# One meta product per block, unread products at the start, and the causal table behind the values' remainder

## The chip, the core and the metric

The kernel runs on one core of a Trainium2 chip. The core has five engines that run side by side, each through its own list of instructions in order: TensorE (PE in the profile, its weight loads PEld), VectorE (DVE), ScalarE (ACT), GpSimd (POOL) and SyncE (SP), which here issues the DMAs. The metric is the device time of one execution in microseconds, as the median of several runs.

## The reference

Two decoder layers over 16 meta tokens and 1024 tokens of width 1024. Each layer normalises its input and projects it to queries, keys, values and gates. One half of the heads does sliding-window attention (window 128; the 16 meta tokens are visible to everyone; a sink logit per head), the other half is an mLSTM, a matrix memory that runs over chunks of tokens. Both are gated, joined and projected back.

```
scores = where(mask, q @ [k_meta, k_band].T * scale, -1e30)
probs  = exp(scores - m) / (sum + exp(sink - m))
ya     = probs @ [v_meta, v_band] * silu(ag)
C_t    = f_t * C_{t-1} + i_t * k_t v_t^T          # mLSTM, per chunk:
S      = q k^T * exp(D - m_t)                     # D is causal: -1e30 above the diagonal
h      = (inter * q C_in + S v) / max(|den|, exp(-m_t))
y      = x + concat(ya, norm(h) * sigmoid(mo) * silu(mgate)) @ w_out
```

The output is the last 1024 tokens, in float32.

## The kernel before, in words

Tokens are cut into nine tiles: tile 0 with the 16 meta tokens, tiles 1 to 8 with 128 tokens each. To keep float32 accuracy, every operand of a large product is split into a high part in the TensorE's rounded format (a copy by ScalarE) and a remainder (a subtraction by VectorE or GpSimd); a product is then three products: high with high, high with remainder, remainder with high (mm3, L196, and the parts at L237).

A layer runs through these stages.

**Start** (kv_tasks). In the first layer the rows of x are loaded tile by tile, squared and summed on ScalarE (first_norm, L340), scaled on VectorE (L298), transposed by TensorE into PSUM (norm_half, L306), copied into H as high part by ScalarE (L310) and as remainder by VectorE (L311). The gain of the norm is spread over all partitions by two products with a row of ones (L504, into two banks G). The four pairs of key and value weights are split on ScalarE (L169) and VectorE (L170). Then each tile is projected (projN, L196).

**Attention** (att_tasks), eight head pairs j by eight blocks b of 128 queries, 64 blocks a layer. A block goes through four steps that are spread over three of its successors: s1 computes the scores of both heads of the pair into S and their softmax into a tile P (ScalarE exponentials at L753, scaling at L758); s2 transposes P with TensorE into the single PSUM bank T: at L775 the 2 x 16 columns that belong to the meta tokens, at L777 the two bands. ScalarE and VectorE split the bands into HL (L784, L786) and the meta part into one of two tiles ptm (L785, L787). s3 starts the output in the single PSUM bank O (L806), s4 adds the meta part with two products of 128 columns, one per head, with weights VM that are zero for the other head's rows (L818), and for b > 1 two products with the differences of neighbouring values (L818, from a band that GpSimd cuts at L797). ScalarE and VectorE then add the halves of O (L825, L827). Between the steps, products of the projections for queries and gates (L237) are woven in by a fixed rule, and the order of TensorE's instructions is pinned to the order in which they are written.

VM is written by v_meta: the values of the meta tokens are copied four times under one another by DMA and multiplied with a column that is one for the rows of a head (hrow).

**Recurrence** (m_tasks), four heads by nine chunks: sa splits the values of a chunk (V, high part at L1015 by ScalarE, remainder at L1016 by GpSimd), turns the keys, updates the state C and computes the decayed scores; the decays come as a table EB by DMA, and mask_eb (L995) adds the causal table tri to one chunk's part of EB on GpSimd. sb and sc_ make the output. Beside it run the projections of the next head. Here a scheduler chooses the order on each engine, from priorities and its own estimate of when things are ready.

**Output projection** (L1324): 16 groups of rows of w_out, streamed in and split.

## Time and profile before

| | before |
|---|---|
| median of 3 runs | 1912.39 us (1911.38 to 1912.49) |
| the profiled execution | 1913.58 us |
| its span in the trace | 1911.9 us |
| TensorE busy | 1892.1 us (99%) |
| VectorE / ScalarE / GpSimd busy | 54% / 55% / 51% |
| instructions | 36057 |

The profile gives each engine's busy time, the chain of work that ended last, groups of instructions by line, and what an engine waited for. A line of the timeline has the start and the length in microseconds, the engine, the line of the kernel, the operation with the tile that it writes and the tiles that it reads, shapes, and how many instructions were merged; in brackets stands how long the engine sat idle before it and who ended that. A product of TensorE lasts longer than the distance to the next one's start, because products overlap.

### The profile page before, as it was taken

How to read it: one execution, taken by the hardware profiler on the slowest of the kernel's cores; microseconds unless marked ns; L12 is line 12 of the kernel's file. 1: busy time of each engine (PE TensorE's matmuls, PEld its weight loads, DVE VectorE, ACT ScalarE, POOL GpSimd, SP SyncE). 2: the span in 40 equal slices, each digit the busy share in tenths (PEclk: the TensorE clock that was granted, in tenths of full speed). 3: DMA queues.
4: the chain of work that ended last, by engine and by line, in shares of the span. 5: the costliest groups of instructions: out<-in, count | busy, mean ns of one | idle time of the engine just before them, and what ended most of it. 6: DMA issues, size and time to landing. Idle time of an engine off the chain costs nothing.

```text
span 1911.9 us, 36057 instructions
## 1 busy us (share of the span) xinstructions
PE 1892.1 (99%) x12779; PEld 1791.3 (94%) x12779; DVE 1035.6 (54%) x2876; ACT 1052.5 (55%) x3131; POOL 984.5 (51%) x1337
## 2 busy tenths in 40 slices
PE   8999999999999999999999999999999999999999
PEld 7999999999999999877789999999999999998887
DVE  8666767657362543443445677675573636336211
ACT  6577877656453544633334778776554545446221
POOL 3665865446545454651325657654565554546342
PEclk9999999999999999999999999999999999999999
DMA  4111111212212221554540111112122121216543
GB/s 156 29 48 44 39 48 50 57 44 56 64 41 64 56 59 45 180 163 157 176 125 23 48 50 35 54 48 56 49 56 60 52 73 35 63 59 204 161 145 131
DMA packets 152422, 148.29 MB, mean 78 GB/s; under 512 B 16665, under 2 KB 125505, under 8 KB 152242
## 3 DMA queue, kind: packets, MB, share of 16 engines
q1 hardware_dynamic: 152242, 145.98, 26.2%
q8 instruction: 101, 1.65, 0.4%
q14 instruction: 79, 0.65, 0.1%
HBM read 122.59 MB, written 23.29 MB: 76 GB/s over the span
## 4 chain that ended last, share of the span: by engine, by line
PE 85%; DVE 4%; DMA 4%; issue 3%; POOL 3%; ACT 2%; SPq 0%; POOLq 0%; ACTq 0%; DVEq 0%
PE pj L196 32%; PE pj L237 22%; PE pss L1324 6%; PE pj L1324 4%; PE po L1324 4%; PE S L731 3%; PE O L818 3%; PE po L1003 2%; PE pss L1003 2%; DMA raw<-in_w_out_dram 2%; PE O L806 2%; PE T L777 1%; PE pj L221 1%; PE pt L1003 1%; DVE t L949 1%
## 5 line engine op out<-in xcount | busy, mean ns | idle before, releaser
L196 PE MATMUL pj<-H,RING 128*128 128x384 f32 (+2 forms) x3312 | 559.4, 322 | 0.3 <-ACT t L967 0.3
L196 PEld LDWEIGHTS pj<-H,RING 128*128 128x128 f32 x3312 | 521.8, 188 | 2.9 <-ACT t L967 0.5
L170 POOL TENSOR_TENSOR RING<-raw,RING 128x512 fp32r<-128x512 f32 (+1 forms) x192 | 255.5, 1335 | 115.1 <-ACT RING L169 112.8
L237 PE MATMUL pj<-RING,H 128*128 128x256 f32 (+1 forms) x1920 | 269.3, 286 | 0.3 <-ACT u L541 0.3
L237 PEld LDWEIGHTS pj<-RING,H 128*128 128x128 f32 x1920 | 242.4, 189 | 0.7 <-ACT u L541 0.6
L237 PE MATMUL pj<-H,RING 128*128 128x384 f32 (+2 forms) x1296 | 239.2, 324 | 0.0
L196 PE MATMUL pj<-RING,H 128*128 128x256 f32 x1536 | 209.6, 287 | 3.9 <-DVE w1k L205 1.8
L237 PEld LDWEIGHTS pj<-H,RING 128*128 128x128 f32 x1296 | 201.1, 188 | 0.0
L196 PEld LDWEIGHTS pj<-RING,H 128*128 128x128 f32 x1536 | 193.7, 191 | 6.3 <-DVE w1k L205 2.2
L188 POOL TENSOR_TENSOR RING<-raw,RING 128x512 fp32r<-128x512 f32 x85 | 110.9, 1311 | 154.6 <-ACT RING L187 137.6
L187 ACT ACTIVATE RING<-raw 128x512 fp32r<-128x512 f32 x128 | 80.8, 633 | 177.6 <-DMA raw<-in_w_out_dram 167.2
L169 ACT ACTIVATE RING<-raw 128x512 fp32r<-128x512 f32 (+1 forms) x196 | 122.6, 626 | 46.1 <-DMA raw<-in_w_in_dram 34.6
L1016 POOL TENSOR_TENSOR p<-u,p 128x258 fp32r<-128x258 f32 x64 | 47.2, 738 | 147.5 <-ACT p L1015 146.0
L797 POOL TENSOR_SCALAR_AFFINE_SELECT p<-p 128x512 fp32r<-128x512 f32 x112 | 71.6, 640 | 96.6 <-DVE p L786 96.2
L1324 PE MATMUL pss<-RING,H 128*128 128x512 f32 x384 | 120.3, 394 | 0.0
L753 ACT ACTIVATE t<-S,mx 128x145 f32<-128x145 f32 x256 | 93.6, 368 | 36.5 <-DVE mx L750 32.0
L1324 PE MATMUL pj<-RING,H 128*128 128x512 f32 x352 | 110.3, 395 | 0.0
L972 DVE SCALAR_TENSOR_TENSOR t<-t,pj 128x384 f32<-128x384 f32 (+2 forms) x48 | 24.6, 512 | 156.8 <-ACT t L971 156.8
L831 POOL TENSOR_TENSOR u<-u,w1k 128x128 f32<-128x128 f32 x128 | 60.3, 471 | 92.2 <-DVE w1k L827 85.1
L949 DVE SCALAR_TENSOR_TENSOR t<-u,cw,t 128x384 f32<-128x384 f32 (+1 forms) x144 | 106.1, 737 | 2.2
L188 DVE TENSOR_TENSOR RING<-raw,RING 128x512 fp32r<-128x512 f32 x43 | 34.6, 806 | 124.5 <-ACT RING L187 124.5
L758 ACT ACTIVATE t<-t,mx 128x144 f32<-128x144 f32 x256 | 91.9, 407 | 4.5 <-DVE mx L755 3.9
(366 smaller groups left out, 3890.3 us busy)
## 6 DMA issues: line engine op xcount, KB each, us to landing
raw<-in_w_out_dram SPq DMA_DIRECT2D x128, 256.0 KB, 3.0
raw<-in_w_in_dram SPq DMA_DIRECT2D x100, 256.0 KB, 2.8
raw<-in_w_in_dram SPq DMA_DIRECT2D x192, 128.0 KB, 2.3
spool<-u SPq DMA_DIRECT2D x56, 192.0 KB, 1.9
p<-x SPq DMA_DIRECT2D x24, 256.0 KB, 3.8
t<-spool SPq DMA_DIRECT2D x30, 192.0 KB, 3.6
p<-spool SPq DMA_DIRECT2D x26, 192.0 KB, 3.6
u<-em SPq DMA_DIRECT2D x8, 576.0 KB, 6.5
```

Source lines behind the costliest of these rows:

```text
L169: sc.activation(hi, raw[:, :, 0:o], AF.Copy)
L170: eng.tensor_tensor(lo, raw[:, :, 0:o], hi, op=ALU.subtract)
L187: sc.activation(hi, raw, AF.Copy)
L188: (eng or (ve if i > 8 and i % 2 else gp)).tensor_tensor(lo, raw, hi, op=ALU.subtract)
L196: last = pin(pe.matmul(out, a, b, start=(i == 0), stop=(i == n - 1)))
L237: pin(pe.matmul(out(), x, y, start=(k + i == 0), stop=(k == n - 1 and i == 2)))
L753: sc.activation(P[:p, 145 * h:145 * h + 145], S[:p, h, 1 + 127 * h:146 + 127 * h], AF.Exp, bias=mx[:p, 0, h:h + 1], accum_out=mx[:p, 1, h: ...
L758: sc.activation(Pn, Pn, AF.Copy, scale=mx[:p, 2, h:h + 1])
L797: gp.affine_select(OW, HL, [[0, 4], [1, 128]], ALU.is_ge, 0.0, base=0, channel_multiplier=-1)
L949: ve.scalar_tensor_tensor(z, RAW[:, t0 + i:t0 + i + n], wcol(i), z, ALU.mult, ALU.add)
L1003: pin(f(*a, **k))
L1324: pin(pe.matmul(ps[:p, :], a, b, start=(i + n == 0), stop=(i == 15 and n == len(terms) - 1)))
```

## The change

Six edits, told in the order of the program.

1. At the start of the first layer seven products are added whose results nobody reads: five of 128 columns with the row of ones ahead of the two that make G, and two copies of those of 512 columns behind them, all into a bank of their own (spare).
2. The four remainders of the first layer's key and value weights are made on GpSimd instead of VectorE.
3. VM holds one weight tile per key head instead of two: the high parts of the values in its left half, the remainders in the right, with the meta values at rows 0 to 15, 32 to 47, 64 to 79 and 96 to 111 and zeros between. The multiplications with hrow go, and so does the clearing of VM.
4. ptm is 256 columns wide, 128 for each head, and zero where a row does not belong to that head. P has a gap of 16 cleared columns between the heads' parts, so that the transposed meta part is 48 rows long, head 0 at rows 0 to 15 and head 1 at 32 to 47. The copy and the subtraction into ptm are done once per head (2 x 16 rows) instead of once (32 rows).
5. In s4 one product of 256 columns takes the place of the two of 128 columns.
6. In sa the causal table is added to the next chunk's decays after the remainder of the present chunk's values, on the same engine, and not before.

```diff
@@ kv_tasks
+                spare = bank("pj")
+                for i in range(5):
+                    pe.matmul(spare[:, 0:128], one, one, start=True, stop=True)
                 for i in range(2):
                     pe.matmul(G[i], one, gr[0:1, 512 * i:512 * i + 512], start=True, stop=True)
+                for i in range(2):
+                    pe.matmul(spare, one, gr[0:1, 512 * i:512 * i + 512], start=True, stop=True)
...
-                             for i in range(4)])
+                             for i in range(4)], gp)
...
-            for i in range(4):
-                ve.tensor_scalar(VM[:, i // 2, i % 2, :], ident, 0.0, None, ALU.mult)
@@ v_meta
-            x = w1k()[0:64, 0:128]
+            x = w1k()[:, 0:128]
+            ve.memset(x, 0.0)
             for i in range(4):
-                sy.dma_start(x[16 * i:16 * i + 16], VR[:16, 0])
+                sy.dma_start(x[32 * i:32 * i + 16], VR[:16, 0])
             vs = x.rearrange("p (v c) -> p v c", v=2)
-            for h in range(2):
-                hi, lo = [VM[0:64, :, h, c:c + 64] for c in (0, 64)]
-                sc.activation(hi, vs, AF.Copy, scale=hrow[0:64, h:h + 1])
-                ve.scalar_tensor_tensor(lo, vs, hrow[0:64, h:h + 1], hi, ALU.mult, ALU.subtract)
+            sc.activation(VM[:, :, 0:64], vs, AF.Copy)
+            ve.tensor_tensor(VM[:, :, 64:128], vs, VM[:, :, 0:64], op=ALU.subtract)
@@ s1
+                ve.memset(P[:, 145:161], 0.0)
@@ s2
-                tm = X[0:32, 256:256 + p]
-                pin(pe.transpose(tm, P[:p, 129:161], ident[:p, :p]))
+                tm = X[0:48, 256:384]
+                pin(pe.transpose(tm, P[:, 129:177], ident))
...
-                    taken = sc.activation(pm[0:32, 0:p], tm, AF.Copy).ins
+                    meta = [(tm[32 * h:32 * h + 16], *(pm[o:o + 16, 128 * h:128 * h + 128]
+                                                       for o in (32 * h, 64 + 32 * h))) for h in range(2)]
+                    for x, hi, lo in meta:
+                        taken = sc.activation(hi, x, AF.Copy).ins
                     ve.tensor_tensor(HL[:, 256:512], X[:, 0:256], HL[:, 0:256], op=ALU.subtract)
-                    ve.tensor_tensor(pm[32:64, 0:p], tm, pm[0:32, 0:p], op=ALU.subtract)
+                    for x, hi, lo in meta:
+                        ve.tensor_tensor(lo, x, hi, op=ALU.subtract)
@@ s4
-                prods = [(VM[:, kv, h, :], pm[:, 0:p], O[:, p * h:p * h + p]) for h in range(2)]
+                prods = [(VM[:, kv], pm, O)]
@@ sa
-                if c < 8:
-                    mask_eb(c + 1)
...
-                gp.tensor_tensor(V[1], v, V[0], op=ALU.subtract)
+                low = gp.tensor_tensor(V[1], v, V[0], op=ALU.subtract).ins
                 if c < 8:
+                    with tc.issue_after(low):
+                        mask_eb(c + 1)
```

The change adds eight lines above the recurrence and the attention, so its line numbers are higher by up to eight than those of the kernel before.

TensorE in the attention of the first layer, one block: the transposes of the meta part and of the bands, the start of the output, woven-in projections (pj), the meta products (from ptm) and the two products with the band differences. Before:

```order
L775 MATMUL T<-cst,t 32x128
L777 MATMUL T<-cst,t 128x128 x2
L806 MATMUL O<-p_1305,u 128x256 x2
L237 MATMUL pj<-H,RING 128x384 x6
L818 MATMUL O<-ptm_105,VM 128x128 x2
L818 MATMUL O<-p_1312,u 128x256 x2
```

and with the change:

```order
L779 MATMUL T<-cst,t 48x128
L781 MATMUL T<-cst,t 128x128 x2
L814 MATMUL O<-p_1318,u 128x256 x2
L237 MATMUL pj<-H,RING 128x384 x6
L826 MATMUL O<-ptm_105,VM 128x256
L826 MATMUL O<-p_1327,u 128x256 x2
```

The block stands at the same place among its neighbours; the two meta products have become one, and the small transpose is 48 rows long.

ScalarE at the start of the first layer, behind the squares of the first tile: the high parts of the weights (RING), squares (po) of the next tile and of the meta tile (16x512), and the copies from the transposes (pt) to H. Before:

```order
L169 ACTIVATE RING_95<-u_134 128x2x256 x2
L310 ACTIVATE H_93<-pt_192 128x4x128
L340 ACTIVATE po_207,nst_206<-u_147 128x512
L340 ACTIVATE po_209,nst_206<-u_147 128x512
L310 ACTIVATE H_93<-pt_199 128x4x128
L340 ACTIVATE po_238,nst_237<-u_149 16x512
```

and with the change:

```order
L169 ACTIVATE RING_95<-u_142 128x2x256 x2
L340 ACTIVATE po_215,nst_214<-u_155 128x512
L340 ACTIVATE po_217,nst_214<-u_155 128x512
L340 ACTIVATE po_242,nst_241<-u_157 16x512
L340 ACTIVATE po_244,nst_241<-u_157 16x512
L310 ACTIVATE H_93<-pt_200 128x4x128
L340 ACTIVATE po_300,nst_299<-u_159 128x512
L340 ACTIVATE po_302,nst_299<-u_159 128x512
L310 ACTIVATE H_93<-pt_207 128x4x128
```

The first copy to H has moved behind the squares of the second and of the meta tile, the second copy behind those of the third. On VectorE the row sums of the meta tile now stand ahead of the scaling of the second tile, and the scaling of the fourth ahead of the last remainder of the second.

GpSimd at the start of the first layer's recurrence: weight remainders (RING), the causal table (tri) added to the decays, the remainders of values and queries (p) and of the state (u). Before:

```order
L170 TENSOR_TENSOR RING<-raw,RING 128x2x256 x4
L995 TENSOR_TENSOR u<-u,tri 128x128 x9
L1016 TENSOR_TENSOR p_6038<-u,p_6038 128x258
L1035 TENSOR_TENSOR p_6037<-u,p_6037 128x128
L1016 TENSOR_TENSOR p_6107<-u,p_6107 128x258
L1050 TENSOR_TENSOR u<-u 128x258
```

and with the change:

```order
L170 TENSOR_TENSOR RING<-raw,RING 128x2x256 x4
L1003 TENSOR_TENSOR u<-u,tri 128x128 x2
L1022 TENSOR_TENSOR p_6170<-u,p_6170 128x258
L1003 TENSOR_TENSOR u<-u,tri 128x128
L1043 TENSOR_TENSOR p_6169<-u,p_6169 128x128
L1022 TENSOR_TENSOR p_6239<-u,p_6239 128x258
```

Nine additions stood in a row ahead of the first full chunk's remainder; now two do, and each further one follows the remainder of a chunk's values.

More of the change, by code (lines that the diff above doesn't have):

```diff
@@ L145, in build @@
     tri = cp.tile([128, 128], F32, name="tri")
-    ptm = [cp.tile([128, 128], F32R, name=f"ptm{i}") for i in range(2)]
+    ptm = [cp.tile([128, 256], F32R, name=f"ptm{i}") for i in range(2)]
     ptm_i = [0]
@@ L372, in parameters2 @@
         for t in ptm:
-            ve.tensor_scalar(t, ident, 0.0, None, ALU.mult)
+            for h in range(2):
+                ve.tensor_scalar(t[:, 128 * h:128 * h + 128], ident, 0.0, None, ALU.mult)
     carry = []
@@ L385, in build @@
         AV, DV = [x[:, 0:896].rearrange("p (t c) -> p t c", t=7) for x in (AV, DV)]
-        VM = sm.tile([128, 2, 2, 128], F32R, name="VM")
+        VM = sm.tile([128, 2, 128], F32R, name="VM")
         KR = unit()[:, :].rearrange("p (t c) -> p t c", t=9)
@@ L752, in s1 @@
                 for h in range(2):
[L753 removed]
+                    sc.activation(P[:p, 161 * h:161 * h + 145], S[:p, h, 1 + 127 * h:146 + 127 * h], AF.Exp,
                                   bias=mx[:p, 0, h:h + 1], accum_out=mx[:p, 1, h:h + 1])
                 ve.reciprocal(mx[:p, 2], mx[:p, 1])
+                ve.memset(P[:, 145:161], 0.0)
                 for h in range(2):
[L757 removed]
+                    Pn = P[:p, 1 + 160 * h:145 + 160 * h]
                     sc.activation(Pn, Pn, AF.Copy, scale=mx[:p, 2, h:h + 1])
@@ L773, in s2 @@
                 blk[1] += 1
-                tm = X[0:32, 256:256 + p]
-                pin(pe.transpose(tm, P[:p, 129:161], ident[:p, :p]))
+                tm = X[0:48, 256:384]
+                pin(pe.transpose(tm, P[:, 129:177], ident))
                 for h in range(2):
-                    pin(pe.transpose(X[:, 128 * h:128 * h + 128], P[:, 1 + 160 * h:129 + 160 * h], ident))
+                    pin(pe.transpose(X[:, 128 * h:128 * h + 128], P[:, 1 + 176 * h:129 + 176 * h], ident))
                 pmeta = live.pop("M") if (j, b) in MRIDE and not last else None
@@ L821, in s4 @@
                 if ride:
-                    pin(pe.matmul(mo[:, 256:384], VM[:, kv, 0, :], pmm, start=True, stop=True))
+                    pin(pe.matmul(mo[:, 256:384], VM[:, kv], pmm, start=True, stop=True))
                 up, y = w1k(), w1k()
```

4 lines of the change are left out of this document (1 added, 3 removed).

## The prediction

> **What bounds the kernel now.** I read the page's table of engines and its chain first, then the table of stretches for the two attention stages, then the list of what TensorE waits for, and last the timeline of single blocks.
>
> ```profile
> span 1911.9 us, 36057 instructions
> ...
> PE 1892.1 (99%) x12779; PEld 1791.3 (94%) x12779; DVE 1035.6 (54%) x2876; ACT 1052.5 (55%) x3131; POOL 984.5 (51%) x1337
> ...
> PE 85%; DVE 4%; DMA 4%; issue 3%; POOL 3%; ACT 2%; SPq 0%; POOLq 0%; ACTq 0%; DVEq 0%
> ```
>
> TensorE is idle for only 19.8 us of the span and makes 85% of the chain, so time is gained where TensorE has less to do, and lost where something makes it wait. The two attention stages, from the table of stretches (busy time of TensorE, its weight loads, VectorE, ScalarE, GpSimd):
>
> ```profile
> 84.00:370.00 286.00, 285.52 (x2229) 282.44 (x2228) 194.74 (x604) 215.92 (x747) 171.88 (x269) 1.00 0.16 45
> ...
> 1040.00:1330.00 290.00, 289.81 (x2256) 287.49 (x2255) 197.57 (x600) 214.52 (x739) 170.78 (x252) 1.00 0.17 47
> ```
>
> TensorE lacks 0.5 and 0.2 us there; ScalarE is 75% busy and VectorE 68%. What TensorE waits for in the whole span, with the causes that the change touches:
>
> ```profile
> PE pt L306 <- DVE u L298: 2.3, 1, 2.3
> ...
> PE pss L1003 <- POOL p L1016: 1.6, 1, 1.6
> ...
> PE po L1003 <- DVE w1k L1067: 1.0, 1, 1.0
> ...
> PE pss L1003 <- DVE w1k L1040: 0.5, 1, 0.5
> ...
> PE T L775 <- DVE ptm L787: 0.4, 2, 0.2
> ```
>
> **The merged product (s4, L818), 128 times.** Two 128-column products with different weights become one 256-column product with one weight tile. The timeline of TensorE around a block with b > 1, one with b = 1, and a long run of 256-column products:
>
> ```profile
> 107.40 0.40 PE L806 MATMUL O<-p,u 128*128 128x256 f32 x2
> 107.63 0.34 PE L818 MATMUL O<-ptm,VM 128*128 128x128 f32 x2
> 107.81 0.45 PE L818 MATMUL O<-p,u 128*128 128x256 f32 x2
> 108.10 2.03 PE L221 MATMUL pj<-RING,HM 128*48 128x256 f32 x16
> ...
> 89.94 0.33 PE L818 MATMUL O<-ptm,VM 128*128 128x128 f32 x2
> 90.11 0.97 PE L237 MATMUL pj<-H,RING 128*128 128x272 f32 x6
> ...
> 55.86 8.80 PE L237 MATMUL pj<-RING,H 128*128 128x256 f32 x72
> 64.50 0.60 PE L442 MATMUL pt<-cst,u 128*128 128x128 f32 x4
> ```
>
> Starts count, not durations, since products overlap. The pair and the two products behind it take 108.10 - 107.63 = 0.47 us, 0.117 for each of four, though two of them are half as wide. The L806 pair takes 0.23 for two, the run 8.64 / 72 = 0.120 for each. So up to 256 columns a product costs a slot of about 0.12 whatever its width: the weight loads set the pace. Three slots make 0.36, so a block with b > 1 saves 0.47 - 0.36 = 0.11, a block with b = 1 0.17 - 0.12 = 0.05. There are 112 and 16: 12.3 + 0.8 = 13.1 us. The starts are rounded to 0.01, and I take 12.6. A page of the Trainium skill speaks against this: TensorE: Matmul & The Clock Gate, Part 2, "Step-by-step: what each phase is for", holds that throughput goes purely by the columns streamed. By it 256 columns cost the same in one piece as in two, and the term would be about nothing; the rows above do not bear that out here, and it is a rival below. The 48-column transpose in place of the 32-column one stands ahead of two 128-column ones and has the slot anyway: nothing.
>
> **The added small work, 128 times.** The halves of the meta probabilities are now copied and subtracted one by one, and a 16-column gap is cleared.
>
> ```profile
> L785 ACT ACTIVATE ptm<-T 32x128 fp32r<-32x128 f32 x128 | 32.2, 251 | 0.0
> ...
> L787 DVE TENSOR_TENSOR ptm<-T,ptm 32x128 fp32r<-32x128 f32 x128 | 35.9, 280 | 3.7
> ...
> L903 DVE MEMSET u<- 128x1 f32 x64 | 2.2, 59 | 0.1
> ```
>
> All run over 128 columns as before, so each extra one costs its full 0.25 on ScalarE and 0.28 on VectorE; the clearing has no row, lies between 0.06 (one column) and 0.28, and I take 0.06, being nearest to 16 columns. Per layer that is 64 x 0.25 = 16 us on ScalarE (to 232 of 286) and 64 x 0.34 = 22 on VectorE (to 217). TensorE's work covers it as long as no buffer that TensorE needs comes back late. There are two single ones: T, which the next transposes need after the last L787, and O, which the next L806 needs after the last L827. The first and the last of the 18 closest meetings on O (18 of 127 neighbouring blocks have a gap under 0.45):
>
> ```profile
> 96.99 0.57 DVE L827 TENSOR_TENSOR w1k<-O,w1k 64x128 f32<-64x128 f32 x2
> 97.75 0.48 PE L806 MATMUL O<-p,u 128*128 128x256 f32 x2
> ...
> 1271.78 0.58 DVE L827 TENSOR_TENSOR w1k<-O,w1k 64x128 f32<-64x128 f32 x2
> 1272.76 0.48 PE L806 MATMUL O<-p,u 128*128 128x256 f32 x2
> ```
>
> The gaps are 0.19 and 0.40; the smallest, five of them, are 0.15, the time of the signal. L827 gets later by what is queued ahead of it: 0.25 to 0.28 if one engine's extra work lies on its path, 0.59 if both do. Adding up over the 127 gaps what a delay of 0.3 leaves uncovered gives 3.3 us; of 0.6, 9.9; of 0.8, 16.5. For T, four gaps are short, and a delay of 0.55 leaves 1.7. I take 3.3 + 1.7 = 5.0 us back, between 0 (the schedule moves the extra work behind L827) and 11.8 (0.6 everywhere).
>
> **The start.** Seven unread products keep TensorE busy while the first data arrive, and GpSimd, not VectorE, makes the first four weight remainders. ScalarE, VectorE, TensorE and GpSimd in the first 24 us:
>
> ```profile
> 9.56 0.60 ACT L310 ACTIVATE H<-pt 128x512 fp32r<-128x512 f32 x1 [0.23 <-PE pt L306]
> ...
> 12.34 0.57 ACT L340 ACTIVATE po<-u 16x512 f32<-16x512 f32 x1
> ...
> 13.57 0.58 ACT L340 ACTIVATE po<-u 128x512 f32<-128x512 f32 x1
> ...
> 12.47 0.69 DVE L311 TENSOR_TENSOR H<-pt,H 128x512 fp32r<-128x512 f32 x1
> 13.08 1.40 DVE L298 SCALAR_TENSOR_TENSOR u<-u,nv,pss 128x512 f32<-128x512 f32 x2
> ...
> 11.69 4.86 PE L196 MATMUL pj<-RING,H 128*128 128x256 f32 x22 [0.69 <-DVE H L311]
> ...
> 19.34 1.69 PE L196 MATMUL pj<-RING,H 128*128 128x256 f32 x12
> ...
> 22.59 0.60 PE L306 MATMUL pt<-cst,u 128*128 128x128 f32 x4
> ...
> L296 POOL TENSOR_TENSOR nv<-nv,cst 128x1 f32<-128x1 f32 x16 | 8.9, 555 | 63.8 <-DVE nv L295 63.7
> ```
>
> The 22 products at 11.69 take 0.22 each, the later ones 0.14 and less, though the table of stretches shows a granted clock of 1.00 in both: early products run at about half pace. If the unread products ended that, the 24 products and 8 transposes would gain some 0.1 each, 3.2 us: the far end. But in the new order ScalarE puts the first copy to H (9.56) behind the squares of the meta tile, which end at about 13.2 as they do now. That is 3.6 us later, with TensorE idle before it: the other end. VectorE comes to its second tile's second half, from 13.2 on, by adding its rows in the new order: row sums 0.3, scaling 1.4, remainder 0.7, meta scaling 1.4, sums and remainder 0.85, sum and remainder 0.85, scaling 1.4, sums and GpSimd's power 0.85, scaling 1.4, remainder 0.7: 23.0. Ten more products of 0.12 end that tile at 24.2, where now tile 3 begins at 22.59: 1.6 later. Behind it TensorE has no gap to make that up. I take +1.6, between -3.2 and +3.6. The same page of the Trainium skill, Part 1, "The HAM clock gate", has the clock at half until a window of about 3.4 us was busy, and again after an idle one. The halved pace agrees with it; by it an idle stretch from 9 to 13.8 us would throw the warm-up away.
>
> **The causal table.** GpSimd adds it nine times in a row as soon as the decays land, ahead of the values' remainder. The start of the second layer's recurrence:
>
> ```profile
> 1365.46 3.83 POOL L995 TENSOR_TENSOR u<-u,tri 128x128 f32<-128x128 f32 x9 [11.34 <-DMA u<-em]
> 1369.25 0.72 POOL L1016 TENSOR_TENSOR p<-u,p 128x258 fp32r<-128x258 f32 x1
> ...
> 1370.03 0.50 PE L1003 MATMUL pss<-p,p 128*128 128x258 f32 x2 [1.60 <-POOL p L1016]
> ```
>
> Now two additions stand ahead of the first remainder instead of nine: it comes seven of 0.42 earlier, 3 us, and the 1.6 us wait goes; the one late after it is L1040, half a microsecond in the first layer. Of the three waits listed (3.1 us) I take 1.8. The moved addition is queued between the remainders, 0.42 in front of the next split of weights, where GpSimd is half idle; if one such delay reaches TensorE per head it costs 8 x 0.42 = 3.4, the bound on the other side.
>
> **The sum.** -12.6 + 5.0 + 1.6 - 1.8 = -7.8 us. The profiled execution took 1913.58 us (span 1911.9 and 1.7 around it); it becomes 1905.8. The median before is 1.2 lower, 1912.39, and so is the forecast: 1904.6 us.
>
> **Rivals.**
> - Full pay: the extra work finds gaps, as TensorE lacks only 0.7 us in both stages, and the start ends even: -12.6 - 1.8 = -14.4, 1898.0. For it: O's gaps are over 0.45 in 109 of 127 blocks. Against it: ScalarE goes from 75 to 81%.
> - No change: L827 is delayed by 0.5, between the sums above 7.5 us, with T 1.5 and the start 1.6: -3.8, 1908.6. It sits on the border of the 0.2% (3.8 us) that a measurement of this kernel can tell from no change.
> - Slower, through O: extra queueing makes the delay of L827 0.8 us. 16.5 + 2.7 on T + 1.6 - 12.6 - 1.8 = +6.4, 1918.8. It decides from a delay of about 0.65, where the waits reach 13. For it: one path holds both engines' extra 0.59; against: a wait at O lets both engines catch up.
> - Columns, not products, set the pace, so the merge brings nothing: +5.0 + 1.6 - 1.8 = +4.8, 1917.2. Speaks against it: 0.47 for four products of mixed width.
> - The unread products bring the whole clock gain, the rest as forecast: -12.6 + 5.0 - 3.2 - 1.8 = -12.6, 1899.8. Against it: ScalarE's order at the start.
>
> **How the numbers follow.** Chances: forecast 0.45, full pay 0.23, no change 0.15, slower through O 0.08, columns 0.03, clock gain 0.06. Faster by over 0.2% holds the forecast, full pay, the clock gain and a small part of the border case: 0.76; slower holds the two that end above: 0.11; 0.13 is left for no difference. The range takes in full pay with half a microsecond of its rounding (13.1 for 12.6) at the low end, and at the high end the border case with the start's upper bound, 2 us more: 1897.5 to 1910.6. Left out are the two slower cases and a little on either side, under 0.2.
>
> **What would show it.** Right: each merged product starts 0.12 ahead of what follows, a step of the attention stages gets about 0.06 shorter on average, and TensorE shows new waits at T and at O behind L827 of some 5 us in all; the first real product starts near 14 us and the attention stage begins over 1 us later; the wait on GpSimd's L1016 is gone. Wrong: the stages shrink by the full 6 us each, or not at all; the waits at O exceed 10 us; or the first 24 us end earlier than now.

## The result

| | before | after |
|---|---|---|
| median | 1912.44 us (1911.38 to 1913.97, 4 runs) | 1926.93 us (1925.87 to 1928.96, 4 runs) |
| ratio | | 1.0071 (95%: 1.0056 to 1.0085) |
| profiled execution (its span) | 1913.58 us (1911.9) | 1926.68 us (1924.9) |

The change makes the kernel slower by 13.6 us; 7.8 us of gain were forecast. A ratio, here and below, is an estimate with its 95% interval and can differ a little from the ratio of the two medians; a price in us is the ratio's distance from 1 times 1912.4.

The head of the page after, the table of stretches for the two attention stages, and the first rows of what TensorE waits for:

```profile
span 1924.9 us, 36207 instructions
PE 1894.0 (98%) x12665; PEld 1785.7 (93%) x12665; DVE 1082.6 (56%) x3122; ACT 1100.5 (57%) x3257; POOL 985.1 (51%) x1341
```

```profile
84.00:370.00 286.00, 277.82 (x2120) 272.36 (x2119) 211.70 (x714) 233.97 (x786) 167.08 (x266) 1.00 0.15 42
1040.00:1330.00 290.00, 286.11 (x2214) 282.61 (x2213) 216.33 (x720) 237.15 (x792) 169.91 (x252) 1.00 0.16 43
```

```profile
PE O L814 <- DVE w1k L835: 4.6, 9, 0.8
PE pj L196 <- ACT t L975: 3.4, 2, 2.3
PE O L814 <- ACT ptm L792: 2.2, 3, 1.0
PE O L814 <- DVE w1k L689: 1.9, 1, 1.9
...
PE O L814 <- DVE t L759: 1.2, 1, 1.2
```

The page counts 114 products fewer on TensorE (128 are merged away, the seven unread ones add 14 records), yet its idle time rose from 19.8 to 30.9 us. In the attention of the first layer it lacks 8.2 us where it lacked 0.5, in that of the second 3.9 where it lacked 0.2. The new waits are at O (L814, L806 before); the other one, at L196, lies in the recurrence.

Where the time went in the two traces, in us. The attention runs from the first transpose at T to the last product at O, the recurrence and the output projection from their first product to their last:

| stage | before | after | difference |
|---|---|---|---|
| up to the first L237 | 49.4 | 53.8 | +4.4 |
| attention, layer 1 and 2 | 298.8, 289.3 | 304.3, 288.1 | +5.5, -1.2 |
| recurrence, layer 1 and 2 | 407.4, 397.3 | 408.5, 401.9 | +1.1, +4.6 |
| output projection, layer 1 | 204.0 | 202.8 | -1.2 |

Together these are 13.2 us; the span grew by 13.0. The merged product itself did what was forecast. The timeline of TensorE around one block with b > 1:

```profile
104.64 0.28 PE L826 MATMUL O<-ptm,VM 128*128 128x256 f32 x1
104.76 0.40 PE L826 MATMUL O<-p,u 128*128 128x256 f32 x2
104.99 1.22 PE L237 MATMUL pj<-H,RING 128*128 128x384 f32 x6
```

Three products in 0.35 us, where four took 0.47. From the first to the last transpose at T of a layer, the distances from these products to the next start add up to 26.2 us before and 20.1 after, in both layers: 12.3 us saved. So the attention stages, 4.3 us longer together, lost 16.6 elsewhere. The groups that the change added or lengthened:

```profile
L795 DVE TENSOR_TENSOR ptm<-T,ptm 16x128 fp32r<-16x128 f32 x256 | 72.9, 285 | 5.5
L792 ACT ACTIVATE ptm<-T 16x128 fp32r<-16x128 f32 x256 | 66.3, 259 | 1.6
...
L759 DVE MEMSET t<- 128x16 f32 x128 | 8.9, 72 | 4.0
```

The mean lengths, 0.285 us for a subtraction, 0.259 for a copy and 0.072 for the clearing, are close to the forecast's 0.28, 0.25 and 0.06. The start, on TensorE:

```profile
8.56 1.91 PE L509 MATMUL pj<-u 1*128 1x512 f32 x2
10.40 1.97 PE L306 MATMUL pt<-cst,u 128*128 128x128 f32 x8
13.41 0.80 PE L196 MATMUL pj<-RING,H 128*128 128x256 f32 x2 [1.04 <-ACT H L310]
15.22 1.11 PE L306 MATMUL pt<-cst,u 128*128 128x128 f32 x4 [1.02 <-DVE H L311]
15.99 3.33 PE L196 MATMUL pj<-RING,H 128*128 128x256 f32 x14
...
25.16 0.60 PE L306 MATMUL pt<-cst,u 128*128 128x128 f32 x4
```

The two last unread products, at 6.85 and 8.56, hold the first transposes up until 10.40 (8.41 before), and tile 3 begins at 25.16 instead of 22.59. From 15.22 to there TensorE has no gap.

### The profile page after: what moved, and what is told of

It reads as the page before. It is cut to its first block, busy times and chain, and to the rows that moved or that the text cites. A ratio compares the mean times of both kernels' runs of the same rounds, so it can differ in the third digit from the quotient of the medians.

```text
span 1924.9 us, 36207 instructions
## 1 busy us (share of the span) xinstructions
PE 1894.0 (98%) x12665; PEld 1785.7 (93%) x12665; DVE 1082.6 (56%) x3122; ACT 1100.5 (57%) x3257; POOL 985.1 (51%) x1341
## 5 line engine op out<-in xcount | busy, mean ns | idle before, releaser
L196 PE MATMUL pj<-H,RING 128*128 128x384 f32 (+2 forms) x3312 | 563.5, 323 | 3.4 <-ACT t L975 3.4
L196 PEld LDWEIGHTS pj<-H,RING 128*128 128x128 f32 x3312 | 524.1, 188 | 7.2 <-ACT t L975 4.3
L170 POOL TENSOR_TENSOR RING<-raw,RING 128x512 fp32r<-128x512 f32 (+1 forms) x192 | 257.2, 1345 | 114.4 <-ACT RING L169 113.2
L237 PE MATMUL pj<-RING,H 128*128 128x256 f32 (+1 forms) x1920 | 268.8, 286 | 0.7 <-ACT u L544 0.7
L237 PEld LDWEIGHTS pj<-RING,H 128*128 128x128 f32 x1920 | 242.5, 189 | 1.1 <-ACT u L544 0.9
L237 PE MATMUL pj<-H,RING 128*128 128x384 f32 (+2 forms) x1296 | 239.0, 324 | 0.0
L196 PE MATMUL pj<-RING,H 128*128 128x256 f32 x1536 | 208.4, 287 | 5.4 <-DVE w1k L205 1.8
L237 PEld LDWEIGHTS pj<-H,RING 128*128 128x128 f32 x1296 | 201.2, 188 | 0.0
L196 PEld LDWEIGHTS pj<-RING,H 128*128 128x128 f32 x1536 | 193.2, 191 | 7.6 <-DVE w1k L205 2.2
L756 ACT ACTIVATE t<-S,mx 128x145 f32<-128x145 f32 x256 | 95.6, 379 | 27.5 <-DVE t L759 17.6
```

Source lines behind the costliest of these rows:

```text
L170: eng.tensor_tensor(lo, raw[:, :, 0:o], hi, op=ALU.subtract)
L196: last = pin(pe.matmul(out, a, b, start=(i == 0), stop=(i == n - 1)))
L237: pin(pe.matmul(out(), x, y, start=(k + i == 0), stop=(k == n - 1 and i == 2)))
L756: sc.activation(P[:p, 161 * h:161 * h + 145], S[:p, h, 1 + 127 * h:146 + 127 * h], AF.Exp, bias=mx[:p, 0, h:h + 1], accum_out=mx[:p, 1, h: ...
```

## The experiments

Each of the 18 kernels ran beside the kernel before on the same chip.

### The three parts alone

Each kernel is the kernel before with some of the six edits, taken from the diff above as they stand there.

**Edits 3 to 5.** 

> The kernel before with edits 3 to 5 alone (one meta product a block, split copies, cleared gap). Theory A (the extra small work makes O come back late): the products save 12.3 us, the waits at O and T give back about 14.7 as they do in the changed kernel, so 1914.8 us, +2.4 on the kernel before, with PE idle some 8 us in the first layer's attention. Rival B (the waits at O come from the other edits, through a shifted schedule): the waits at O stay near the 5 us of the prediction, and the time is 1905.

Measured: 1917.8 us, ratio 1.0028 (1.0017 to 1.0039), +5.4 us. Theory A: the waits are those of the changed kernel,

```profile
PE O L809 <- DVE w1k L830: 2.4, 5, 0.8
PE O L809 <- ACT ptm L787: 2.0, 2, 1.0
PE O L809 <- DVE w1k L684: 1.9, 1, 1.9
```

here of the first layer's attention (microseconds, times, longest): for the additions from O (L830), for the small copy (L787), and once, 1.9 us, at a head's end (L684). The other edits have no part in them.

**Edits 1 and 2.** 

> The kernel before with edits 1 and 2 alone (unread products, weight remainders on GpSimd). Theory A: the end of the start comes 4.4 us later, as in the changed kernel, and nothing makes that up: 1916.8 us. Rival B: the loss at the start is no more than the 1.6 us predicted, and the rest of it comes from the other edits: 1914.0. Rival C: the start is early but ends even, 1912.4.

Measured: 1915.5 us, ratio 1.0012 (1.0003 to 1.0021), +2.3 us. Its first L237 begins at 51.81 us, 2.4 later than before, so the loss at the start reaches the end. It lies between A and B.

**Edit 6.** 

> The kernel before with edit 6 alone (the causal table behind the remainder of the values). Theory A: it is this edit that makes the second layer's recurrence 4.6 us and the first layer's 1.1 us longer: 1918.1 us. Rival B: the longer recurrence comes from a changed order elsewhere, and this edit gains the 1.8 us predicted: 1910.6.

Measured: 1917.3 us, ratio 1.0020 (1.0011 to 1.0029), +3.8 us. The second layer's recurrence takes 400.0 us in its trace, 2.8 more than before, the first layer's 407.2, 0.2 less. So A holds for the second layer and in its sign, and the forecast gain of 1.8 us fails. The trace is that of the fastest run, 1914.76 us, and its span is only 1.2 us longer than the one before; most of the slower runs have a lower mean granted clock (last section). The timeline around the longest new wait:

```profile
1414.37 1.25 DVE L949 SCALAR_TENSOR_TENSOR t<-u,cw,t 128x384 f32<-128x384 f32 x1
...
1415.62 0.73 POOL L1014 TENSOR_TENSOR p<-Vm,p 16x258 fp32r<-16x258 f32 x1
1415.66 2.75 DVE L949 SCALAR_TENSOR_TENSOR t<-u,cw,t 128x384 f32<-128x384 f32 x1
...
1416.33 0.45 POOL L995 TENSOR_TENSOR u<-u,tri 128x128 f32<-128x128 f32 x1
...
1416.74 1.25 POOL L170 TENSOR_TENSOR RING<-raw,RING 128x512 fp32r<-128x512 f32 x1
1418.44 0.52 ACT L951 ACTIVATE t<-t 128x384 f32<-128x384 f32 x1 [2.23 <-DVE t L949]
1418.87 0.37 ACT L967 ACTIVATE t<-pj 128x256 f32<-128x256 f32 x1
...
1419.29 0.97 PE L196 MATMUL pj<-H,RING 128*128 128x384 f32 x4 [2.33 <-ACT t L967]
```

The moved addition (L995) stands between a remainder and a split of weights, and GpSimd works from 1415.62 to 1417.99 without a gap. Beside it one instruction of VectorE lasts 2.75 us; ScalarE's tanh waits for it, the next tanh in ScalarE's list behind that, and TensorE for that one, 2.33 us.

### Is it the bank O?

The changed kernel, with O as one tile of 512 columns whose halves the blocks use in turn:

```
-                live["O"] = bank("O")
-                O = live["O"][:, 0:256]
+                o0 = 256 * (turn_o[0] % 2)
+                turn_o[0] += 1
+                live["O"] = OO[:, o0:o0 + 256], OO[:, 256 - o0:512 - o0]
+                O = live["O"][0]
```

> The changed kernel with O in two halves of one bank that blocks use in turn, so that a block's output start no longer waits for the addition of the block in front; the added copies, subtractions and clearings stay. Theory A (waits at O, 16.5 us in both layers, of which 3.3 were there before): these go, and at most a few us appear at T and P: 1911 to 1915 us. Rival B: the delay is in VectorE and ScalarE as a whole, and the waits move from O to T, S or the band differences: 1921 or more. Rival C: writing one half of a bank while the other is read costs TensorE time: over 1927.

Measured: 1928.3 us, ratio 1.0081 (1.0067 to 1.0095). The waits are where they were, since the writes to one half are still ordered behind the reads of the other, and so this tells none of the three theories apart. An addition from O and the next block's start, in the timeline:

```profile
102.72 0.57 DVE L837 TENSOR_TENSOR w1k<-O,w1k 64x128 f32<-64x128 f32 x2
...
103.44 0.47 PE L816 MATMUL O<-p,u 128*128 128x256 f32 x2 [0.69 <-DVE w1k L837]
```

The block at 103.44 writes the half that L837 doesn't read, and starts 0.15 us behind it all the same. That is as the Trainium skill has it (PSUM — Partial Sum Buffer, "PSUM bank collisions raise a hardware error"): two engines may not touch one bank in the same partitions at once, whatever the columns, and the software has to order them.

### Which of the added instructions?

The next four kernels are edits 3 to 5 without the clearing, with one or two copies (ScalarE) and one or two subtractions (VectorE) a block:

```
-                    for x, hi, lo in meta:
+                    for x, hi, lo in meta[:1]:
                         taken = sc.activation(hi, x, AF.Copy).ins
                     ve.tensor_tensor(HL[:, 256:512], X[:, 0:256], HL[:, 0:256], op=ALU.subtract)
-                    for x, hi, lo in meta:
+                    for x, hi, lo in meta[:1]:
                         ve.tensor_tensor(lo, x, hi, op=ALU.subtract)
```

**One and one.** 

> Edits 3 to 5 alone, with the meta part of the second head left out: one copy and one subtraction a block, on 16 rows, and no clearing of the gap, so as many small instructions as in the kernel before. Theory A (the added small work makes O and T late, the merged product itself pays): the 12.3 us of the products come in full, the waits at O fall back to the 3.3 us of before, 1900.6 us. Rival B (the merge makes TensorE arrive earlier and the saving turns into waits by itself): 1906 or more, with waits at O of over 5 us.

Measured: 1901.9 us, ratio 0.9945 (0.9932 to 0.9957), -10.5 us: theory A. TensorE's only row at O in the whole span:

```profile
PE O L808 <- DVE w1k L829: 0.9, 2, 0.4
```

**Two copies, one subtraction.** 

> As the kernel with the second head's meta part left out, but ScalarE's copy is done for both heads; VectorE's subtraction still for one, no clearing. Theory A1 (VectorE may not read bank T while ScalarE reads it, as its subtraction of the bands waits for the last meta copy, so one more copy delays all that VectorE has to do behind it): over half of the 17 us between 1900.6 and the 1917.8 of edits 3 to 5, about 1910. Rival A2 (only the engine with the work is delayed; VectorE's own subtraction, just ahead of the additions from O, is what counts): 1903 to 1905.

Measured: 1914.1 us, ratio 1.0011 (1.0002 to 1.0020), +2.1 us: the one copy costs 12.6 us. The rows at O are back:

```profile
PE O L808 <- DVE w1k L829: 4.6, 9, 1.2
...
PE O L808 <- ACT t L751: 1.9, 1, 1.9
...
PE O L808 <- ACT ptm L786: 1.6, 3, 1.0
```

**One copy, two subtractions.** 

> As the kernel with the second head's meta part left out, but VectorE's subtraction is done for both heads; ScalarE's copy for one, no clearing. Theory A1: the smaller part of the 17 us, about 1906. Rival A2: the larger part, 1911 to 1913.

Measured: 1903.2 us, ratio 0.9956 (0.9943 to 0.9968), -8.4 us. The one subtraction costs 2.1 us, less than either theory had and hardly more than two such runs can tell apart.

**Two and two, no clearing.** 

> Edits 3 to 5 with both heads' copies and subtractions, without the clearing of the gap (its rows are read by nobody). Theory A (copies and subtractions make the waits; the clearing adds 0.07 us of VectorE): 1916 to 1918, as with the clearing, 1917.8. Rival M (the exponentials wait for the clearing on VectorE's list, 17.6 us in 16 waits, and that is what delays ScalarE): 1908 or less.

Measured: 1918.8 us, ratio 1.0037 (1.0024 to 1.0049), +7.1 us, against +5.4 with the clearing. Theory A: the clearing costs nothing that can be seen. Beside two copies the second subtraction costs 5.0 us (7.1 against 2.1), so the two prices do not simply add. In the trace of the changed kernel the exponentials wait 17.6 us for it in all,

```profile
L756 ACT ACTIVATE t<-S,mx 128x145 f32<-128x145 f32 x256 | 95.6, 379 | 27.5 <-DVE t L759 17.6 <-DVE mx L753 7.0
```

but these are the waits for the row maxima (mx) under another name: the clearing follows a maximum on VectorE's list and takes 0.07 us, and in the kernel without it the exponentials wait 23.9 us for the maxima themselves.

### By which path does the copy act?

**Moved to VectorE.** From the kernel with two and two, the second head's copy:

```
+                    x, hi, lo = meta[1]
+                    ve.tensor_copy(hi, x)
+                    ve.tensor_tensor(lo, x, hi, op=ALU.subtract)
```

> Edits 3 to 5 complete but for the clearing, with the second head's meta copy moved from ScalarE to VectorE, behind the subtraction of the bands: ScalarE has one small copy a block as before the change, VectorE one copy and one subtraction more (0.56 us). Theory A1 (the extra copy on ScalarE delays VectorE's reading of bank T, and the delay runs on through the exponentials and the copy from O; extra work on VectorE behind the subtraction costs little): the 1903.2 of the kernel with two subtractions and one copy, plus the 1 to 2 us that a further small VectorE instruction cost there: about 1905, faster than both kernels. Rival A3 (what counts is the sum of the small work on the two engines): 1914 or more.

Measured: 1912.7 us, ratio 1.0000 (0.9992 to 1.0009). Neither: A1's 1905 is out by 8 us, so VectorE is not free either. One instruction of 0.28 more costs it 2.1 us, two cost 10.5. The waits are now at T:

```profile
PE T L773 <- DVE ptm L791: 3.0, 2, 1.7
```

**Not from bank T.** From the kernel with two copies and one subtraction:

```
-                        taken = sc.activation(hi, x, AF.Copy).ins
+                        taken = sc.activation(hi, x if x is meta[0][0] else HL[32:48, 0:128], AF.Copy).ins
```

> As the kernel with two copies and one subtraction (1914.1 us), but ScalarE's second small copy reads the copied bands in SBUF and not bank T; its place on ScalarE's list and its length stay (the second head's high part so holds other data). Theory A1 (the bank: VectorE's subtraction of the bands waits for all of ScalarE's reads of T): VectorE starts that subtraction 0.28 us earlier again, and the time falls to 1903 to 1907. Rival A4 (ScalarE's own list: the exponentials and the copy from O stand behind the extra copy, whatever it reads): 1912 to 1915.

Measured: 1913.1 us, ratio 1.0001 (0.9992 to 1.0009). The time is A4's. VectorE's subtraction of the bands does start earlier, at 0.24 us behind the copy of the bands (median of 128) as with one copy, where it was 0.52 with two copies from T; but that brings 1.9 us, about what two such runs can tell apart. ScalarE's copy from O starts 0.78 us behind the last product into O with one small copy, 1.06 with two from T, 1.17 with the second from SBUF (medians). So the second copy is dear through ScalarE's own list too, without a wait of VectorE at T. The run does not divide the 12.6 us between the two paths, though, as neither the copy's length nor its place stayed: from SBUF it takes 0.31 us instead of 0.26, and in 69 of the 128 blocks other work of ScalarE, mostly exponentials, comes between the two copies, where with two from T they stand side by side in every block.

**Without the merge.** The kernel before, its copy L785 made twice:

```
+                    sc.activation(pm[0:32, 0:p], tm, AF.Copy)
                     taken = sc.activation(pm[0:32, 0:p], tm, AF.Copy).ins
```

> The kernel before with ScalarE's copy of the meta part made twice, to the same place, and nothing else. Theory A (the copy's 0.28 us on ScalarE's list delays the output bank by more than its own length): 12 us, as the second copy cost beside the merged product, 1924. Rival E (only the saving makes it dear, as TensorE now comes 0.11 us earlier in each block): 1916 to 1918.

Measured: 1929.6 us, ratio 1.0086 (1.0072 to 1.0100), +16.4 us. So a second copy is dear without the merge too, against E. The path is another, though, so this does not show A. A block on ScalarE and VectorE:

```profile
108.50 0.25 ACT L785 ACTIVATE ptm<-T 32x128 fp32r<-32x128 f32 x1
108.91 0.38 ACT L753 ACTIVATE t<-S,mx 128x145 f32<-128x145 f32 x1 [0.16 <-DVE mx L750]
...
109.64 0.25 ACT L786 ACTIVATE ptm<-T 32x128 fp32r<-32x128 f32 x1
...
109.98 0.42 DVE L787 TENSOR_TENSOR p<-T,p 128x256 fp32r<-128x256 f32 x1
```

The second copy has come behind the exponentials, and VectorE's subtraction of the bands (L787), which doesn't need it, waits for it as both read T. So here it is T that comes back late (8.3 us in nine waits of TensorE for L788), and the wait of one engine for the other at bank T does act.

### The full computation without the copy

In these three, ScalarE and VectorE split the meta part in one piece of 32 rows as before, into a side tile sg, and GpSimd spreads it over the heads' columns:

```
+                    gp.tensor_tensor(pm[0:64].rearrange("p (h c) -> p h c", h=2),
+                                     sg.rearrange("p (h c) -> p h c", h=1).to_broadcast([64, 2, 128]),
+                                     hrow[0:64].rearrange("p (h c) -> p h c", c=1).to_broadcast([64, 2, 128]),
+                                     op=ALU.mult)
```

**One tile ptm.** 

> The merged product fed in another way: the meta part is transposed, copied and subtracted in one piece of 32 rows as before the change, into a side tile, and GpSimd spreads it over the two heads' columns with one multiplication by the head's mask (64x256, some 0.7 us a block); no added work on ScalarE or VectorE. Theory A1: ScalarE's and VectorE's lists are as before, GpSimd goes from 60% to some 76% and has a whole block's time for it: 1900 to 1903. Rival G (GpSimd's 45 us more a layer slow VectorE, as its instructions of up to 2.75 us beside GpSimd's rows suggest, or make the band differences late): 1908 or more.

Measured: 2211.5 us, ratio 1.1554 (1.1538 to 1.1571). It tells nothing of the theories: in the program the next block's spread stands ahead of the present block's product, so that with one tile the product takes the next block's data and TensorE waits for GpSimd in 117 blocks, 222.5 us, at a mean granted clock of 0.97.

**Two halves of a tile, products of 64 rows.** 

> The merged product with the full computation: one copy and one subtraction of 32 rows into a side tile as before the change, and GpSimd spreads them over the two heads' columns with one multiplication by the heads' mask (64x256, about 0.6 us), into two halves by partitions of one tile; no clearing, no added work on ScalarE or VectorE. Theory A1: TensorE saves the 12.3 us, the waits at O stay at 3 to 4, and the time is 1900 to 1904. Rival G (GpSimd's 39 us a layer make the band differences or the gated outputs late, or slow VectorE): 1908 or more.

Measured: 1953.0 us, ratio 1.0216 (1.0199 to 1.0233). The waits at O were 1.1 us in both attention stages together, but the products got dear:

```profile
109.00 0.39 PE L809 MATMUL O<-p,u 128*128 128x256 f32 x2
109.33 0.38 PE L821 MATMUL O<-ptm,VM 64*128 64x256 f32 x1
109.64 0.51 PE L821 MATMUL O<-p,u 128*128 128x256 f32 x2
109.98 2.05 PE L221 MATMUL pj<-RING,HM 128*48 128x256 f32 x16
```

The product of 64 rows is 0.31 us ahead of the next, the one before it 0.21, the one behind it 0.22, where 0.12 is usual: 0.385 us too much a block, 49 us in all.

**Two tiles, products of 128 rows.** The side tile lies in columns that DV does not use. 

> The merged product with the full computation, spread by GpSimd as in the kernel before this one, but with products of 128 rows, the lower half zero, and two tiles ptm in turn. That one lost 0.19 us in each 64-row product and 0.2 us in its neighbours, 0.385 us a block or 49 us in all, of its 1953; without that it is 1904. Theory A1 (ScalarE's list unchanged): 1900 to 1904, faster than both kernels, with waits at O and for ptm of some 3 us. Rival G (GpSimd's 39 us a layer cost as much as ScalarE's copies): 1910 or more.

Measured: 1909.7 us, ratio 0.9984 (0.9975 to 0.9993), -3.1 us. The merge pays with the full computation, and this version beats both kernels, by less than A1's 8 to 12 us; rival G is nearer. What costs the rest is not shown: GpSimd has 78 us more to do, but of TensorE's waits at T and O only 1.2 us name its ptm, and 2.5 us VectorE's subtraction into the side tile (L785):

```profile
PE T L773 <- DVE u L785: 2.5, 5, 0.8
...
PE O L808 <- DVE w1k L829: 1.2, 2, 0.7
PE O L820 <- POOL ptm L786: 1.2, 3, 0.8
```

### The start and the table once more

**Edit 1 alone.** 

> The kernel before with edit 1 alone (the seven unread products). Theory S1 (the two 512-column copies stand ahead of the first transposes on TensorE and run at half pace, so they delay the first tile by what the whole start lost): the first transposes come 3 us later as with edits 1 and 2, the start ends 3 us later, 1915. Rival S2 (the later start comes from ScalarE's and VectorE's order, which edit 2 changes): 1912.

Measured: 1914.5 us, ratio 1.0006 (0.9997 to 1.0015).

**Edit 2 alone.** 

> The kernel before with edit 2 alone (the four weight remainders on GpSimd). Theory S1: TensorE's first transposes stay at their time; VectorE is freed of four remainders, the start ends up to 1 us earlier: 1911.5 to 1912.5. Rival S2: GpSimd's slower remainders (1.3 us against 0.7) or the changed order make the first products late: 1914 to 1916.

Measured: 1915.5 us, ratio 1.0008 (0.9999 to 1.0017). The times tell neither from no change. The traces do: with edit 1 alone the first transposes begin at 10.40 us as in the changed kernel, with edit 2 alone at 7.82. It is the unread products that hold them up (S1). The first L237 begins at 51.36 us with edit 1 alone, at 49.33 with edit 2 alone (49.38 before) and at 51.81 with both, so edit 1 makes 2.0 of the 2.4 us by which the start got longer.

**The additions on VectorE**, in the order of edit 6 and in that of before (in mask_eb, ve.tensor_tensor for gp.tensor_tensor).

> Edit 6 alone, with the moved additions of the causal table on VectorE instead of GpSimd; they stand at the same place of the program. Theory P (VectorE's three-operand instructions of the convolution stand still beside GpSimd's work; a GpSimd row without a gap made one 2.75 us long, and ScalarE and TensorE waited behind it): the mean of that instruction falls below the 0.89 us of edit 6 alone, the 2.3 us wait of TensorE in the second layer goes, 1911 to 1913. Rival O (tying the addition to the remainder changes the order of the lists, whoever does it): the wait stays, 1915 or more.

Measured: 1934.8 us, ratio 1.0111 (1.0096 to 1.0127).

> The kernel before with the additions of the causal table on VectorE, in the order of before. Theory P: GpSimd is rid of 41 us, so VectorE's instructions beside it get shorter by more than the 72 additions of 0.28 us cost it, and TensorE's 1.6 us wait for the remainder goes: 1910 to 1912. Rival O: nine additions in a row on VectorE delay its list, 1914 or more.

Measured: 1931.3 us, ratio 1.0111 (1.0091 to 1.0131). P fails as a forecast in both. O's bounds, 1915 and 1914 or more, were met, but not for its reason: the two orders differ by less than the runs can tell, so what costs is that VectorE has the additions.

```profile
L949 DVE SCALAR_TENSOR_TENSOR t<-u,cw,t 128x384 f32<-128x384 f32 x96 | 75.0, 781 | 1.4
...
L995 DVE TENSOR_TENSOR u<-u,tri 128x128 f32<-128x128 f32 x72 | 27.8, 442 | 9.0 <-DMA u<-em 9.0
```

In the kernel with edit 6's order (these rows) the mean of L949 is 0.78 us; with edit 6 on GpSimd it is 0.83, in the kernel before 0.76. So it falls as P has it, by 0.05, but the 72 additions of 0.44 on VectorE cost more, and TensorE waits for VectorE and ScalarE in new places; the 2.3 us wait itself is gone, the longest for the same tanh (L967) is 1.4. A part is the clock: the mean granted clock of the ten runs was 0.994 to 0.998, and in the trace of the first kernel it fell in five places. By its mean of 0.996 that is some 8 of 1933 us, an estimate. That GpSimd's row lengthens the one instruction of 2.75 us is read from the trace and not shown by these runs.

## Why the prediction was wrong

**What bounds the kernel**: right. The times follow TensorE's waits and its number of products, nearly in order, and to within 4.8 us. Add up, for the first product at O and at T in each block, what its distance to the product in front exceeds the usual one by (where over 0.06 us):

| edits 3 to 5, and variants | waits at O | at T | -12.3 + (O + T - 3.2) | measured |
|---|---|---|---|---|
| kernel before | 0.8 | 2.4 | | |
| one copy, one subtraction | 2.1 | 2.3 | -11.1 | -10.5 |
| one copy, two subtractions | 3.9 | 2.8 | -8.8 | -8.4 |
| spread by GpSimd, 128 rows | 4.6 | 5.1 | -5.8 | -3.1 |
| second copy on VectorE | 6.4 | 8.6 | -0.5 | 0.0 |
| two copies, one from SBUF | 11.2 | 3.9 | -0.4 | +0.2 |
| two copies, one subtraction | 12.5 | 3.2 | +0.2 | +2.1 |
| two and two | 13.9 | 3.9 | +2.3 | +7.1 |
| edits 3 to 5 as they are | 14.4 | 3.9 | +2.8 | +5.4 |
| changed kernel | 14.5 | 3.9 | | |

**The merged product** (-12.6 us): right, 12.3 us. That a product of up to 256 columns costs a slot of about 0.12 us holds, and the Trainium skill's rule weighed against it in the prediction (TensorE: Matmul & The Clock Gate, Part 2, "Step-by-step: what each phase is for"), throughput purely by columns, does not: by it the kernel with one copy and one subtraction would not have gained its 10.5 us.

**The added small work** (+5.0 us): this is the step that failed. The prediction summed what a delay leaves uncovered over the gaps at O and had 3.3 us for 0.3, 9.9 for 0.6 and 16.5 for 0.8, and took 0.3: "0.25 to 0.28 if one engine's extra work lies on its path". The waits at O and T rose by 15.2 us; the whole price, from one and one to two and two, was 17.6. What was wrong is the delay. From the end of the additions from O to the next block's first product the median gap was 1.25 us before, 1.19 with one and one, 0.75 with two copies; gaps of under 0.17, where TensorE waits, went from 5 before to 7 and 31 of 127. So one copy of 0.26 us brought O back 0.44 later. Part of it is ScalarE's list (its copy from O starts 0.28 later); how much is bank T, where VectorE's subtraction starts 0.28 later, and what else adds to the 0.44 stays open. And a uniform delay was the wrong picture: some waits at heads' ends are 1.9 us. ScalarE's spare quarter of the stage was an average: of the 33 us that 128 second copies of 0.26 take, 12.6 came out in the time. The subtraction, last in VectorE's turn, cost 2.1 us beside one copy and 5.0 beside two.

**The rival "slower, through O"** had 0.08 and was the right mechanism with nearly the right size: 16.5 + 2.7 us of waits, of which 14.5 + 3.9 came. Its condition, a delay of over 0.65, was not met; the price was reached at half a microsecond. Waits at O of over 10 us were also the sign of being wrong that the prediction named.

**The start** (+1.6 us): the sign was right, the size not: +2.4 in its trace alone, +4.4 in the changed kernel. The late first copy to H came as said (first product at 13.41 us, 14 said). The prediction did not count that the unread products stand ahead of the first transposes, which they delay by 2 us. And it let VectorE's list set the end of the second tile, 24.2 us; but from 15.22 to 25.16 TensorE had no gap, and it ran at half pace until 20.6 us, where before it was at full pace from 16.3. Of the 2 us more that the changed kernel's start loses than edits 1 and 2 alone, 0.6 are there by tile 3 (with those two edits full pace comes at 18.8 us), and 1.3 are longer waits of TensorE for a remainder of VectorE (L311, 1.1 us against 0.5) and ahead of the first L237 (0.7 against none). Why is open.

**The causal table** (-1.8 us): wrong sign, +3.8 us. The wait for the first remainder did shrink (1.6 to 0.9 us with edit 6 alone, 0.6 in the changed kernel). The bound on the other side, 3.4 us by "one such delay per head", had the size, but in the trace the delay came at one place, through VectorE and ScalarE, and a part of the 3.8 us goes with a lower granted clock in six of the eleven runs (last section).

The three parts alone make 5.4 + 2.3 + 3.8 = 11.5 of the 13.6 us; the start's further 2 us would be the rest, which no run tests.

## What to carry to other kernels

Before adding an instruction to an engine that is "75% busy", follow the loop that returns the buffer TensorE waits for, and price the instruction by each engine that it passes through, not by its length against an average of spare time; where the trace has gaps close to nothing, a few tenths more can eat the saving of every block. A merged product is worth its slot (0.12 us here), so feed it without new work on the engines of that loop: with GpSimd's help it brought 3 us, with one more ScalarE copy nothing.

## What the runs showed of the hardware

**Half pace at the start.** Products on one row, the unread ones and those of G, from 1.14 to 10.40 us without a gap, did not end it: the products at 15.99 start 0.21 us apart, and full pace (0.12) comes at 20.6 us, 4.6 behind the first of them. In the kernel before it comes at 16.3 us, 4.6 behind the start of the products at 11.69. The rule weighed in the prediction (the Trainium skill, TensorE: Matmul & The Clock Gate, Part 1, "The HAM clock gate"), a busy window of some 3.4 us, is not met by such products here. The table of stretches shows a granted clock of 1.00 throughout:

```profile
0.00:10.00 10.00, 8.86 (x18) 4.62 (x18) 3.79 (x17) 5.14 (x9) 3.77 (x8) 1.00 0.78 256
...
13.00:20.00 7.00, 5.57 (x25) 5.28 (x26) 6.38 (x15) 3.87 (x11) 1.36 (x3) 1.00 0.90 364
```

**A fall of the clock after a wait.** In the changed kernel's second recurrence the 2.3 us wait (the one shown for edit 6) was followed by a granted clock of 0.57, and 18 products took 0.27 us each, 1.5 us more in all; in the profiled run of the kernel with edit 6 alone the same wait was followed by products of 0.18 at a granted clock of 1.00.

```profile
1428.00:1430.00 2.00, 0.89 (x5) 0.89 (x6) 1.83 (x11) 1.36 (x4) 0.40 (x1) 1.00 0.49 123
1430.00:1432.00 2.00, 2.00 (x9) 2.00 (x8) 1.01 (x6) 1.54 (x6) 0.41 (x3) 0.57 0.04 12
1432.00:1434.00 2.00, 2.00 (x9) 1.97 (x8) 0.84 (x2) 0.66 (x2) 1.41 (x3) 0.58 0.00 0
```

The columns are those of the stretches, the granted clock third from the end. Whether the clock falls seems to differ from run to run: of the 11 runs with edit 6 alone, the five with a mean granted clock of 1.000 took 1914.76 to 1917.37 us (median 1915.45), the six with 0.999 took 1916.88 to 1918.27 (median 1917.8). By an estimate from these rows, one such fall (4 us at 0.57) lowers the mean of 1925 us by 0.001. What decides it is not shown.

**VectorE beside GpSimd.** Of the 144 instructions of L949 in the kernel before, the 57 that no GpSimd instruction overlaps take 0.60 us (median), and 21 during which one begins take 0.61. Of the 35 that start with 0.4 us or more of a GpSimd instruction still to run (the one-column ones, L1077 and L1078, not counted), 34 end a fixed time behind it, 0.41 us with 384 columns and 0.30 with 272: one that starts 1.12 us before the end of a weight remainder (L170) takes 1.53. The 2.75 us one of edit 6 ended 0.42 us behind the last of the row's three. The Trainium skill (SBUF — State Buffer, the table of terms, "shared port pair") has the two engines share a port that one holds for a whole instruction while the other stands still; the trace agrees.

**Rows of a product.** A product of 64 rows between products of 128 costs, with its two neighbours, 0.385 us more than the three slots of 0.12 that they take with 128 rows.
